# Group 0's convolutions three GLU tiles behind, with four shifted operands, and three gate pairs before their branches

## The chip, the cores and the metric

One Trainium2 chip, a program on all eight cores, each with its own 2048 prompt tokens and 64 sample tokens, no exchange between cores. The time of a run is that of its slowest core, in device microseconds. Most runs agree within 0.3%, but some fall in a slower state, in which the cores of one die or both show a lower granted clock; only fast runs are compared for whole times.

A few words before the rest. **PE** is TensorE, **DVE** VectorE, **ACT** ScalarE, **SP** SyncE, which here does nothing but issue copies. **Stages** below are read from each core's trace, all eight cores, by the end of four instructions of group 0: the last write of the GLU output of tile 0 ("glu 0"), the last convolution matmul ("conv 7"), the last tile of the gated mixture ("mix") and the last residual sum of the output projection ("projection"). The profile page itself is that of the slowest core alone.

## The reference, cut to what matters

One decoder layer. Attention and a causal depthwise convolution run side by side on the same normalised input; sigmoid gates merge them; an output projection adds to the residual; an MLP follows.

```python
q, k, v, u, g = _project(_rmsnorm(x, norm1_g), w_in, b_gate)   # u = ua * sigmoid(ub): GLU, 1024 channels
ya = _prompt_attention(q, k, v, sink)
c = conv31(pad(u)) + conv_b                                    # 31 taps, one filter per channel
yc = silu(layernorm(c)) @ w_conv_o
mix = (g0 * (ya @ w_attn_o) + g1 * yc) @ w_out
h = x + mix
h = h + square(relu(rmsnorm(h) @ w_up)) @ w_down
```

## The kernel before: the parts that the argument touches

Tokens are split in three groups; group 0 has 640 columns. Only there the convolution runs on PE (later groups do it on DVE behind the MLP). A channel tile of 128 is cut in four quarters q of 32 channels. For each quarter, 32 partitions of `um` are copied to four places, shifted by i = 0 to 3 columns; eight matmuls of 128 rows and 32 columns then sum 32 taps. That takes 16 small SBUF-to-SBUF copies for each tile, all issued by SP.

```python
GROUPS = [(0, 5, 128, 0), (5, 6, 0, 0), (11, 5, 0, NSMP)]
M_OUT = list(range(8)) + [10, 11, 14, 15, 8, 9, 12, 13]      # order of the output projection's tiles
ush = [over(X[1], i * 8 * ULEN, f"ush{i}", [128, 4, ULEN], BF16) for i in range(2)]   # shifted operands
cw = [over(H, 4096 + i * 2048, ...) for i in range(2)]                                # taps
um = [over(H, 8192 + i * 2560, ...) for i in range(2)]                                # GLU output
tAH = over(H, 8 * HB, "tAH", [128, 4, WMAX], F32)            # gates held for two pairs, in H's tiles 8-11
tBH = over(H, 12 * HB, "tBH", [128, 4, WMAX], F32)           # and 12-15

def glu(m):
    ...
    if first:
        P.dma("sp", cw[m % 2][...], cwb[:, m, :]..., f"d_cw{m % 2}")
    ...                                   # 64 matmuls, Tanh on ACT, multiply on DVE into um[m % 2]
    if first:
        z = ush[m % 2]
        for i in range(4):
            for q in range(4):
                P.dma("sp", z[32 * i:32 * i + 32, q, 0:L - 3], u[32 * q:32 * q + 32, i:i + L - 3],
                      f"d_ul{m % 2}{i}{q}", merge=(i + q > 0))
...
for m in range(8):
    glu(m)
    if first and m >= 1:
        conv(m - 1)
...
if first:
    side.extend([lambda: None, lambda: None, lambda: conv(7), lambda: None, lambda: ln_stats(0)])
    side.extend([lambda m=m: ln_apply(0, m, cf[m % 2]) for m in range(8)])
```

`side` is a list of small tasks; after each gate chunk (16 matmuls, 2.17 us) one is taken. In the gates of group 0 the tasks are, first, the last conv and the layer norm; then, when those are done, the squares of group 1's input (16 loads of 384 KB through the three-tile ring `xrP`) and the residual loads into H:

```python
if first:
    for p in range(2):
        gate(p, tA, 0)
        gate(p, tB, 16)
    drain()                                                   # runs what is left in side
    begin, tasks = norm1_squares(g + 1, xrP)
    begin()
    side.extend(tasks)                                        # 33 tasks
    side.extend([lambda m=m: load_res([m]) for m in M_OUT[:12]])   # 12 tasks
    for p in range(2):
        branches(p)
for p in range(2 if first else 0, 8):
    gate(p, tA, 0); gate(p, tB, 16); branches(p)
drain()
begin, tasks = norm1_scale(g + 1, XF[...], xrP)               # reads the same 16 tiles again, during
begin()                                                       # the output projection, into the ring
side.extend(tasks)
if first:
    load_res(M_OUT[12:])
```

The helper that ends the program makes SP wait for every semaphore that the program ever used:

```python
def emit(self):
    fin = [(s, v) for s, v in self.cnt.items() if v > 0]
    self.streams["sp"].append((fin, None, None))
```

The softmax here doesn't subtract the row's maximum and nothing guards it: scores larger than these inputs give would overflow.

## Time and profile before

| | before |
|---|---|
| time, median of 4 runs | 3396.76 us (3395.22 to 3692.71; the longest run was slow) |
| cores of the profiled run | 3373.6 to 3390.5 us |
| PE busy | 3312.6 of 3390.5 us |
| conv stage (glu 0 to conv 7), median of cores | 122.8 us (115.0 to 137.5) |
| to the last mix tile | 207.1 us |
| output projection | 78.6 us (71.3 to 79.8) |

The page of the slowest core (4): busy time of PE, the granted clock in 40 slices, and the chain that ended last.

```profile
PE 3312.6 (98%) x22688; PEld 2161.1 (64%) x22688; DVE 1621.9 (48%) x2438; ACT 718.6 (21%) x1371; POOL 267.9 (8%) x475
PEclk7989999999999999999999999999999999999999
...
PE 94%; DMA 2%; DVE 2%; SPq 1%; issue 1%; ACT 0%; DVEq 0%; ACTq 0%; POOLq 0%
```

PE is the bound. A slice is 85 us long; the two with a clock under nine tenths are the first and the third (170 to 254 us). The table of stretches of the same core shows where: columns are the stretch, its length, busy us and instruction counts of each engine, the clock, the share of the DMA engines.

```profile
core 4: us, PE busy (x) PEld busy (x) DVE busy (x) ACT busy (x) POOL busy (x), PEclk, DMA share, GB/s
144.00:166.00 22.00, 18.28 (x161) 10.54 (x161) 11.08 (x10) 8.37 (x18) 6.32 (x11) 0.92 0.55 119
...
182.00:206.50 24.50, 15.95 (x184) 10.24 (x176) 7.40 (x8) 3.44 (x7) 0.53 (x1) 0.79 0.75 151
206.50:241.00 34.50, 25.88 (x261) 16.71 (x256) 5.95 (x10) 5.82 (x12) 1.05 (x2) 0.85 0.62 117
241.00:275.00 34.00, 27.98 (x273) 18.30 (x271) 6.94 (x11) 8.08 (x15) 1.06 (x2) 0.90 0.44 98
```

PE's waits between 120 and 275 us (total us, times, longest) and two conv lines of its timeline:

```profile
PE ps L157 <- DMA ush_89<-um_95: 22.7, 6, 6.7
PE ps L157 <- DMA ush_88<-um_94: 3.0, 1, 3.0
...
202.54 4.12 PE L157 MATMUL ps<-ush_89,cw_93 128*32 128x320 bf16 x61 [6.66 <-DMA ush_89<-um_95]
...
215.82 2.37 PE L157 MATMUL ps<-ush_88,cw_92 128*32 128x320 bf16 x64
```

The same conv takes 2.37 us when PE was busy before it; after a wait, its last 61 of 64 matmuls alone take 4.12 us. The timeline of SP shows why PE waits: a set of 16 shifts takes 11 to 13 us to issue, one GLU's matmuls take 9.3.

```profile
181.94 12.55 SPq L157 DMA_DIRECT2D ush_89<-um_95  x16
194.64 0.47 SPq L157 DMA_DIRECT2D cw_92<-cwb  x1
195.41 11.26 SPq L157 DMA_DIRECT2D ush_88<-um_94  x16
```

### The profile page before, as it was taken

The numbers are of one execution on the slowest core, as the hardware profiler recorded it, in microseconds if no ns is written. First come the engines' busy times: TensorE is split into PE (matmuls) and PEld (weight loads), VectorE is DVE, ScalarE is ACT, GpSimd is POOL, SyncE is SP. The second block draws the span as 40 slices with busy tenths as digits, with TensorE's granted clock in tenths as the row PEclk, the third lists the DMA queues.
The fourth block names the chain that finished last, engine by engine and source line by source line (L and its number), as shares of the span: only waits on it lengthen the run. The fifth ranks groups of instructions, "written<-read, shape, count | busy, mean of one in ns | idle before, by whom it ended". The sixth has DMA issues, their size and how long they took to land.

```text
span 3390.5 us, 59039 instructions; the slowest of 8 cores (3373.6 to 3390.5 us)
## 1 busy us (share of the span) xinstructions
PE 3312.6 (98%) x22688; PEld 2161.1 (64%) x22688; DVE 1621.9 (48%) x2438; ACT 718.6 (21%) x1371; POOL 267.9 (8%) x475
## 2 busy tenths in 40 slices
PE   6979999999999999999999999999999999999998
PEld 4556776567777775666655666666666666666667
DVE  4534333668889453225288666644542232222225
ACT  2323223321211222112242020203211230101022
POOL 0200000300000000000130000000000000000000
PEclk7989999999999999999999999999999999999999
DMA  6766997467776696858648655555778656668651
GB/s 150 143 119 135 194 188 153 84 123 140 139 142 119 118 197 141 191 110 177 123 83 158 114 102 104 104 102 112 156 165 194 111 110 112 112 109 150 109 106 70
DMA packets 88770, 446.79 MB, mean 132 GB/s; under 512 B 11024, under 2 KB 19920, under 8 KB 45648
## 3 DMA queue, kind: packets, MB, share of 16 engines
q0 software_dynamic: 48240, 349.36, 57.3%
q1 hardware_dynamic: 39968, 93.12, 9.1%
q8 instruction: 187, 3.06, 0.4%
q14 instruction: 87, 0.71, 0.1%
q10 hardware_dynamic: 288, 0.52, 0.0%
HBM read 766.65 MB, written 25.94 MB: 234 GB/s over the span
## 4 chain that ended last, share of the span: by engine, by line
PE 94%; DMA 2%; DVE 2%; SPq 1%; issue 1%; ACT 0%; DVEq 0%; ACTq 0%; POOLq 0%
PE ps L157 94%; SPq L157 1%; DMA ush_89<-um_95 1%; DVE rden_68 L157 0%; DMA wsl_49<-wst 0%; DVE rden_67 L157 0%; DVE H L157 0%; DMA xs_106<-xp 0%; DMA xrP_121<-x 0%; DMA xs_107<-xp 0%; DMA xs_105<-xp 0%; DMA ush_88<-um_94 0%; ACT TQ L157 0%; DVE XF_79 L157 0%; DVE XQ_84 L157 0%
## 5 line engine op out<-in xcount | busy, mean ns | idle before, releaser
L157 DVE TENSOR_TENSOR H<-ps,H 128x320 f32<-128x320 f32 (+4 forms) x400 | 202.7, 507 | 378.1 <-PE ps L157 377.9
L157 PE MATMUL ps<-XF_79,wsl_49 128*128 128x320 bf16 (+3 forms) x1568 | 243.2, 312 | 11.8 <-DVE XF_79 L157 6.3
L157 PE MATMUL ps<-XF_79,wsl_53 128*128 128x320 bf16 (+2 forms) x1472 | 219.6, 309 | 0.0
L157 PE MATMUL ps<-XF_79,wsl_52 128*128 128x320 bf16 (+2 forms) x1472 | 219.4, 310 | 0.0
L157 PE MATMUL ps<-XF_79,wsl_50 128*128 128x320 bf16 (+2 forms) x1472 | 217.7, 308 | 0.8 <-DVE XF_79 L157 0.5
L157 PEld LDWEIGHTS ps<-XF_79,wsl_49 128*128 128x128 bf16 x1568 | 155.1, 99 | 97.0 <-issue 26.4
L157 PE MATMUL ps<-XF_81,wsl_49 128*128 128x384 bf16 (+2 forms) x1344 | 210.2, 317 | 0.0
L157 PE MATMUL ps<-XF_81,wsl_52 128*128 128x384 bf16 (+2 forms) x1344 | 206.0, 314 | 0.0
L157 PE MATMUL ps<-XF_81,wsl_50 128*128 128x384 bf16 (+2 forms) x1280 | 200.0, 317 | 0.0
L157 PE MATMUL ps<-XF_79,wsl_51 128*128 128x320 bf16 (+2 forms) x1344 | 197.8, 307 | 0.0
L157 PE MATMUL ps<-XF_81,wsl_53 128*128 128x384 bf16 (+2 forms) x1280 | 197.4, 315 | 0.0
L157 PEld LDWEIGHTS ps<-XF_79,wsl_53 128*128 128x128 bf16 x1472 | 143.5, 98 | 73.0 <-issue 2.7
L157 PEld LDWEIGHTS ps<-XF_79,wsl_52 128*128 128x128 bf16 x1472 | 143.7, 98 | 72.1 <-issue 1.4
L157 PEld LDWEIGHTS ps<-XF_79,wsl_50 128*128 128x128 bf16 x1472 | 143.4, 98 | 71.7 <-issue 4.0
L157 PE MATMUL ps<-XF_81,wsl_51 128*128 128x384 bf16 (+2 forms) x1216 | 186.5, 314 | 0.0
L157 PEld LDWEIGHTS ps<-XF_81,wsl_49 128*128 128x128 bf16 x1344 | 132.0, 98 | 74.6 <-issue 0.4
L157 DVE SCALAR_TENSOR_TENSOR tAP<-tAP,ps 128x384 f32<-128x384 f32 (+1 forms) x64 | 34.4, 537 | 302.5 <-PE ps L157 301.6
L157 PE MATMUL ps<-XF_80,wsl_49 128*128 128x352 bf16 (+4 forms) x1184 | 178.8, 311 | 0.0
L157 PEld LDWEIGHTS ps<-XF_81,wsl_52 128*128 128x128 bf16 x1344 | 131.3, 98 | 71.3 <-issue 1.0
L157 PEld LDWEIGHTS ps<-XF_79,wsl_51 128*128 128x128 bf16 x1344 | 131.1, 98 | 63.7 <-issue 2.1
L157 PEld LDWEIGHTS ps<-XF_81,wsl_50 128*128 128x128 bf16 x1280 | 125.6, 98 | 71.3 <-issue 1.4
L157 PE MATMUL ps<-XF_80,wsl_51 128*128 128x352 bf16 (+4 forms) x1120 | 170.6, 313 | 0.0
(406 smaller groups left out, 4575.5 us busy)
## 6 DMA issues: line engine op xcount, KB each, us to landing
wsl_49<-wst POOLq DMA_DIRECT2D x66, 1024.0 KB, 8.2
wsl_50<-wst POOLq DMA_DIRECT2D x66, 1024.0 KB, 8.3
wsl_51<-wst POOLq DMA_DIRECT2D x65, 1024.0 KB, 8.3
wsl_52<-wst POOLq DMA_DIRECT2D x65, 1024.0 KB, 8.2
wsl_53<-wst POOLq DMA_DIRECT2D x65, 1024.0 KB, 8.1
xrP_121<-x SPq DMA_DIRECT2D x18, 384.0 KB, 7.6
xrP_123<-x SPq DMA_DIRECT2D x18, 352.0 KB, 5.4
H<-x SPq DMA_DIRECT2D x16, 384.0 KB, 10.2
```

The source lines that it names most:

```text
L157: i = getattr(eng, ins[0])(**ins[1])
```

## The change

Its intent: let conv m run after glu m+3 instead of after glu m+1, so that the shifts have two more GLUs to arrive. That needs four shifted operands (each now cut to `UL0`, group 0's own 672 columns, where `ULEN` was 1248); taps are asked for later, so that they do not hold up shifts on SP; convs 5, 6 and 7 move into the gates; and to have room for them, a third gate pair is done before the branches, with six instead of four gate slots, which changes the order in which H's tiles come free (`M_OUT`).

```diff
-M_OUT = list(range(8)) + [10, 11, 14, 15, 8, 9, 12, 13]
+M_OUT = [0, 1, 2, 3, 6, 7, 8, 9, 12, 13, 14, 15, 4, 5, 10, 11]
-        ush = [over(X[1], i * 8 * ULEN, f"ush{i}", [128, 4, ULEN], BF16) for i in range(2)]
+        ush = [over(X[1], i * 8 * UL0, f"ush{i}", [128, 4, UL0], BF16) for i in range(4)]
... (um likewise of length UL0)
-        tAH = over(H, 8 * HB, "tAH", [128, 4, WMAX], F32)
-        tBH = over(H, 12 * HB, "tBH", [128, 4, WMAX], F32)
+        tAH = over(H, 4 * HB, "tAH", [128, 6, WMAX], F32)
+        tBH = over(H, 10 * HB, "tBH", [128, 6, WMAX], F32)
... (the order of the weight slabs follows the gates)
+            def load_taps(m):
+                P.dma("sp", cw[m % 2][:, :, :, :], cwb[:, m, :]..., f"d_cw{m % 2}")
             def glu(m):
-                if first:
-                    P.dma("sp", cw[m % 2]...)
+                if first and m >= 2:
+                    load_taps(m - 2)
...
-                    z = ush[m % 2]
+                    z = ush[m % 4]
-                                  f"d_ul{m % 2}{i}{q}", merge=(i + q > 0))
+                                  f"d_ul{m % 4}{i}{q}", merge=(i + q > 0))
...     in conv(m), after its matmuls:
+                if m in (4, 5):
+                    load_taps(m + 2)
...
-                if first and m >= 1:
-                    conv(m - 1)
+                if first and m >= 3:
+                    conv(m - 3)
...
-                side.extend([lambda: None, lambda: None, lambda: conv(7), lambda: None, lambda: ln_stats(0)])
+                side.extend([lambda: None] + [lambda m=m: conv(m) for m in (5, 6, 7)] + [lambda: None, lambda: ln_stats(0)])
...     in gates:
-                for p in range(2):
+                for p in range(3):
                     gate(p, tA, 0)
                     gate(p, tB, 16)
                 drain()
                 begin, tasks = norm1_squares(g + 1, xrP)
...
-                for p in range(2):
+                for p in range(3):
                     branches(p)
-            for p in range(2 if first else 0, 8):
+            for p in range(3 if first else 0, 8):
```

More of the change, by code (lines that the diff above doesn't have):

```diff
@@ L23 @@
 SEQW = 36
-M_OUT = list(range(8)) + [10, 11, 14, 15, 8, 9, 12, 13]
+M_OUT = [0, 1, 2, 3, 6, 7, 8, 9, 12, 13, 14, 15, 4, 5, 10, 11]
 NK = 14
 NB = 46
-ULEN = 32 + 640 + 16 * SEQW
+UL0 = 32 + 128 * GROUPS[0][1]
 NSLOT = 5
@@ L253, in build @@
         XU = [over(X[i], 4 * HB, f"XU{i}", [128, 8, WMAX + 32], BF16) for i in range(3)]
-        ush = [over(X[1], i * 8 * ULEN, f"ush{i}", [128, 4, ULEN], BF16) for i in range(2)]
+        ush = [over(X[1], i * 8 * UL0, f"ush{i}", [128, 4, UL0], BF16) for i in range(4)]
         gtH = [over(H, i * 2048, f"gtH{i}", [128, 512], F32) for i in range(2)]
         cw = [over(H, 4096 + i * 2048, f"cw{i}", [128, 4, 8, 32], BF16) for i in range(2)]
-        um = [over(H, 8192 + i * 2560, f"um{i}", [128, ULEN], BF16) for i in range(2)]
-        tAH = over(H, 8 * HB, "tAH", [128, 4, WMAX], F32)
-        tBH = over(H, 12 * HB, "tBH", [128, 4, WMAX], F32)
+        um = [over(H, 8192 + i * 2560, f"um{i}", [128, UL0], BF16) for i in range(2)]
+        tAH = over(H, 4 * HB, "tAH", [128, 6, WMAX], F32)
+        tBH = over(H, 10 * HB, "tBH", [128, 6, WMAX], F32)
         KcT = over(X[1], 0, "KcT", [128, 2, 16, 128], BF16)
@@ L300, in bank @@
             return bank() if b in held else b
-        A, B, C = range(NK), range(NK, NB), range(NB, 110)
+        A, C = range(NK), range(NB, 110)
+        B1 = [NK + i for i in (0, 1, 2, 3, 6, 7, 4, 5, 8)] + [*range(NK + 9, NB)]
         B2 = [NK + i for i in (0, 1, 4, 2, 3, 5)] + [*range(NK + 6, NB)]
-        order = [*A, *B, *A, *C, *B2, *A, *C, *B2, *C][:-3]
+        order = [*A, *B1, *A, *C, *B2, *A, *C, *B2, *C][:-3]
         nxt = [0]
@@ L806, in front @@
             L = 32 + Mp
+            def load_taps(m):
+                P.dma("sp", cw[m % 2][:, :, :, :], cwb[:, m, :].rearrange("p (b t c) -> p b t c", b=4, t=8),
+                      f"d_cw{m % 2}")
             def glu(m):
@@ L810, in glu @@
                 wl = slab()
-                if first:
-                    P.dma("sp", cw[m % 2][:, :, :, :], cwb[:, m, :].rearrange("p (b t c) -> p b t c", b=4, t=8),
-                          f"d_cw{m % 2}")
-                else:
+                if first and m >= 2:
+                    load_taps(m - 2)
+                if not first:
                     P.op("act", "copy", out=u[:, 0:32], in_=cuT[:, m, :])
@@ L846, in glu @@
                             P.dma("sp", z[32 * i:32 * i + 32, q, 0:L - 3], u[32 * q:32 * q + 32, i:i + L - 3],
-                                  f"d_ul{m % 2}{i}{q}", merge=(i + q > 0))
+                                  f"d_ul{m % 4}{i}{q}", merge=(i + q > 0))
             def conv(m):
-                z = ush[m % 2]
+                z = ush[m % 4]
                 c_w = cw[m % 2]
@@ L942, in gate @@
                         b = fm(w, j, nT, halo + c0, n)
-                        act(t[:, jj % 4 if first and p < 2 else j, c0:c0 + n], b[:, 0:n], AF.Tanh, scale=0.5,
+                        act(t[:, jj % 6 if first and p < 3 else j, c0:c0 + n], b[:, 0:n], AF.Tanh, scale=0.5,
                             bias=hbg[:, bias + jj:bias + jj + 1])
@@ L950, in branches @@
                     jj = 2 * p + j
-                    i = jj % 4 if first and p < 2 else j
+                    i = jj % 6 if first and p < 3 else j
                     f = slice(j * 128, j * 128 + 128)
```

## The prediction

> **What bounds it.** TensorE: the busy table gives PE 98% of 3390.5 us, the chain of waits 94%. The change can win only where PE stands or runs at a low clock. Group 0's GLU/convolution stage holds most of that: in the table of stretches PE is busy 18.3 of 22.0 us (144-166 us), 16.0 of 24.5 (182-206.5), 25.9 of 34.5 (206.5-241) and 28.0 of 34.0 (241-275), at granted clocks of 0.92, 0.79, 0.85, 0.90. In the list of PE's waits, the shifted operands (ush) account for 22.7 + 3.0 us.
>
> **Cause.** Each conv(m) follows glu(m+1), 9.3 us of matmuls. Its 16 shift copies take 11.0 to 13.3 us to issue on SP (timeline, mean 12.2), and the last lands 3.8 to 8.5 us later. Every second conv therefore waits, then runs cold: 64 matmuls take 4.1 to 5.9 us instead of 2.37. The Trainium skill, "TensorE: Matmul & The Clock Gate", Part 1, says an idle window of about 3.4 us halves the clock; this trace agrees (0.58 at 202-207 us, 0.57 at 230-242).
>
> **What the change does.** It lets conv lag three GLUs behind, with four ush buffers. No operation count changes. Three gate pairs precede their branches, to make room for conv 5, 6, 7 after gate chunks of 2.17 us each.
>
> **Gain without waits.** From 145.0 us (end of glu 1), glu 2 and 3 with attention take about 24 us; five convs (2.35) and four glus (9.25) then end at 218. Four gate chunks and conv 5 to 7 end at about 233.5. Before reaches that point at 270.9 + 2.2 = 273.1. So 39.6 us is the ceiling.
>
> **What takes half of it back.** SP does not get faster. From 133.6 us it must issue 8 sets x 12.2 us plus six tap loads at 0.7: the last shift is issued near 236. The taps of conv 6 are asked for only after conv 4, in program order behind the last shifts, so conv 6 has no taps and conv 7 no operands until about 242.5, an estimate from landings of 3.1 to 9.4 us. PE arrives at 226.8 us: one wait of about 16 us, on cw, then a cold restart (about 5 us for conv 6). Conv 7 ends near 252.5 us, 20.5 us earlier than now. Two um buffers make DVE wait in glu 5 to 7 (2 to 5 us each); eight PSUM banks absorb that.
>
> **Later.** Side tasks: 45 against 40 steps (48 before), so five residual loads are drained at the gates' end. SP can start the 12 loads (34.9 us) about 48 us before the output projection, so nothing is given back there. The last normalised tile is already just in time (0.5 us PE wait at 549 us), so up to 2 us could appear.
>
> **Predicted:** 3396.6 - 20.5 = 3376 us, 80% range 3362 to 3387. Chances: faster by over 2% 0.01; within 2% 0.98; slower 0.01.
>
> **What would show it.** SP's shift sets back to back; conv 0 to 5 with no PE wait, about 2.37 us each; one long PE wait at conv 6 released by the cw DMA; conv 7's end near 252 us; the rest unchanged and shifted.
>
> **What would make it wrong.** Issue time: at 10.5 us per set the gain is about 33 us, at 13.5 about 10. Conv 6 not waiting would mean the taps' order is harmless. A PE wait on PSUM banks in glu 6 or 7 would mean the two um buffers matter. A wait on H or XF at 450-560 us would be a give-back.

## The result

3400.51 us (median of 4 runs, 3399.25 to 4015.05; the longest was slow) against 3396.76. The ratio is 1.0011, 95% interval 0.9989 to 1.0034: the same. A ratio is the mean time of one kernel's fast runs over that of the other's of the same rounds, so it is not quite the ratio of the medians. I had predicted 3376, with a range of 3362 to 3387.

So nothing was gained; yet in the conv stage the trace looks much as predicted. On the profiled core (7) the waits for shifts are gone (on the other seven too: PE's only waits for copies there are for taps, 4.5 to 6.9 us in all), the clock holds until 206 us, and the last conv ends at 252.1 us; I had said 252.5. First the stretches, then SP's timeline (sets back to back), then PE's waits between 120 and 260 us.

```profile
core 7: us, PE busy (x) PEld busy (x) DVE busy (x) ACT busy (x) POOL busy (x), PEclk, DMA share, GB/s
144.00:166.00 22.00, 21.02 (x148) 12.04 (x146) 16.54 (x14) 8.53 (x19) 8.20 (x15) 1.00 0.67 118
...
182.00:206.50 24.50, 22.55 (x243) 14.86 (x241) 5.95 (x10) 5.38 (x11) 1.06 (x2) 1.00 0.76 149
206.50:241.00 34.50, 28.05 (x313) 18.36 (x311) 5.95 (x10) 6.94 (x14) 1.06 (x2) 0.91 0.76 145
```

```profile
189.51 11.89 SPq L157 DMA_DIRECT2D ush<-um  x16
201.55 0.47 SPq L157 DMA_DIRECT2D cw<-cwb  x1
202.53 11.32 SPq L157 DMA_DIRECT2D ush<-um  x16
214.00 0.47 SPq L157 DMA_DIRECT2D cw<-cwb  x1
```

```profile
PE ps L157 <- DMA cw<-cwb: 6.7, 2, 5.6
```

The one long wait left is for taps (5.6 us), before conv 5, and that conv then takes 5.83 us cold (granted clock 0.50 from 235.8 to 241.7 us). Conv 5 and conv 7:

```profile
235.84 5.83 PE L157 MATMUL ps<-ush,cw 128*32 128x320 bf16 x64 [5.60 <-DMA cw<-cwb]
...
249.74 2.37 PE L157 MATMUL ps<-ush,cw 128*32 128x320 bf16 x64
```

Where did the gain go? Stages of all cores:

| stage, median of 8 cores (range), us | before | after |
|---|---|---|
| start to glu 0 | 132.5 | 133.5 |
| glu 0 to conv 7 | 122.8 (115.0 to 137.5) | 116.0 (114.8 to 118.7) |
| to the last mix tile | 207.1 (207.1 to 207.2) | 204.7 (204.7) |
| output projection | 78.6 (71.3 to 79.8) | 91.7 (86.8 to 95.8) |
| last 635 us (from group 2's projection to the end) | 634.0 (633.5 to 635.1) | 635.8 (635.6 to 636.3) |
| end, median of cores | 3383.1 | 3390.4 |

Two things stand out. The conv stage gained not 20.5 but 6.8 us in the median, plus 2.4 us in the next row, most of it a gate chunk that now comes before conv 7: 9.2 us together. The 137.5 us was core 4 alone, the very core whose page I had read. And the output projection lost 13.1 us. PE's waits between 440 and 580 us, before (core 4) and after (core 7):

```profile
PE ps L157 <- DVE XF_79 L157: 0.5, 1, 0.5
```

```profile
PE ps L157 <- DVE XF L157: 9.3, 3, 3.9
PE ps L157 <- DVE H L157: 6.3, 1, 6.3
```

PE waits for DVE, and DVE waits for loads: the chain of waits of the new kernel from 443 us shows two `xrP` loads that take 21 and 29 us, one after the other, where the ring has three tiles (start, length, what).

```profile
443.83 21.08 DMA xrP<-x
...
466.12 28.81 DMA xrP<-x
...
495.98 0.49 DVE H L157
...
496.72 26.25 PE ps L157 x176
```

In the old kernel the loads of this time (issued from 15 us before the last mix tile to 30 us after it) landed in 4 to 18 us on all cores. The one load that stands in its chain, near the end of the projection (core 4):

```profile
538.24 9.72 DMA xrP_121<-x
```

SP's issues and PE's first projection matmuls say when each kernel asks for its loads, before (core 4), then after (core 7):

```profile
401.96 0.33 SPq L157 DMA_DIRECT2D xrP_121<-x  x1
402.34 34.87 SPq L157 DMA_DIRECT2D H<-x  x12
...
473.77 13.89 SPq L157 DMA_DIRECT2D H<-x  x4
...
476.56 8.86 PE L157 MATMUL ps<-XF_80,wsl_52 128*128 128x320 bf16 x64
```

```profile
406.93 0.33 SPq L157 DMA_DIRECT2D xrP<-x  x1
407.31 36.33 SPq L157 DMA_DIRECT2D H<-x  x12
443.83 1.54 SPq L157 DMA_DIRECT2D xrP<-x  x3
452.58 7.07 SPq L157 DMA_DIRECT2D H<-x  x4
...
455.44 34.94 PE L157 MATMUL ps<-XF,wsl 128*128 128x320 bf16 x256
```

The stretches from the residual loads to the projection tell what differs, before (core 4) and after (core 7); the last but one figure is the DMA share.

```profile
402.00:438.00 36.00, 36.00 (x262) 25.69 (x261) 13.61 (x17) 11.95 (x20) 2.11 (x4) 1.00 0.97 218
438.00:474.00 36.00, 36.00 (x268) 25.93 (x266) 9.10 (x19) 5.50 (x11) 2.11 (x4) 1.00 0.85 176
474.00:510.00 36.00, 36.00 (x268) 25.93 (x266) 18.99 (x36) 10.42 (x19) 2.11 (x4) 1.00 0.97 202
```

```profile
407.00:443.00 36.00, 36.00 (x262) 25.71 (x260) 13.44 (x17) 11.90 (x20) 2.11 (x4) 1.00 0.94 200
443.00:457.00 14.00, 14.00 (x105) 10.09 (x104) 5.81 (x12) 1.24 (x3) 1.05 (x2) 1.00 1.01 214
457.00:497.00 40.00, 33.66 (x248) 24.01 (x247) 10.64 (x19) 7.02 (x13) 2.11 (x4) 0.97 1.01 215
```

Both kernels fill the DMA engines while the twelve residual loads run, and again during the projection. Before, 36 us at a share of 0.85 lay between the two. After, the last mix tile comes 14 us after the last of the twelve was issued, and the engines stay full for over 50 us.

A full share alone does not make loads slow: in the old kernel it is 1.03 from 498 to 518 us (core 4), and the loads issued there landed in 7.5 to 11.3 us. What differs is the backlog. 10 us before the last mix tile, the loads that SP had issued and that had not landed were 0 or 1 on every core before, and 4 to 7 after; 10 us after that tile they were 2 or 3 before, and 4 to 7 after.

### The profile page after: what moved, and what is told of

The parts are those of the page before. It is cut to its first block, busy times and chain, and to the rows that moved or that the text cites. A ratio compares the mean times of both kernels' runs of the same rounds, so it can differ in the third digit from the quotient of the medians.

```text
span 3398.2 us, 59063 instructions; the slowest of 8 cores (3378.2 to 3398.2 us)
## 1 busy us (share of the span) xinstructions
PE 3316.6 (98%) x22688; PEld 2161.8 (64%) x22688; DVE 1622.8 (48%) x2438; ACT 718.7 (21%) x1371; POOL 267.8 (8%) x475
## 4 chain that ended last, share of the span: by engine, by line
PE 90%; DMA 3%; SPq 3%; DVE 2%; issue 1%; ACT 0%; DVEq 0%; ACTq 0%
PE ps L157 90%; SPq L157 3%; DMA xrP<-x 2%; DMA H<-x 1%; DVE rden L157 1%; DMA vec<-vecs 1%; DVE H L157 0%; DVE XF L157 0%; DMA cw<-cwb 0%; ACT TQ L157 0%; DVE R L157 0%; DVE XQ L157 0%; ACT tI L157 0%; DVE wpr L157 0%; SPq L154 0%
## 5 line engine op out<-in xcount | busy, mean ns | idle before, releaser
L157 PE MATMUL ps<-XF,wsl 128*128 128x384 bf16 (+4 forms) x19392 | 2909.9, 312 | 28.7 <-DVE XF L157 20.2
L157 PEld LDWEIGHTS ps<-XF,wsl 128*128 128x128 bf16 x19392 | 1892.3, 98 | 1043.4 <-issue 66.2
L157 DVE SCALAR_TENSOR_TENSOR acc<-XU,vec,acc 128x768 f32<-128x768 bf16 (+1 forms) x480 | 440.1, 946 | 1.1 <-ACT acc L157 1.1
L157 ACT ACTIVATE XF<-rt 128x320 bf16<-128x320 f32 (+2 forms) x384 | 189.8, 496 | 1129.9 <-DVE rt L157 1129.8
L157 POOL DMA_DIRECT2D wsl<-wst x327 | 173.5, 531 | 2900.4 <-PE ps L157 2839.3
L157 DVE SCALAR_TENSOR_TENSOR rt<-ps,LM 128x320 f32<-128x320 f32 (+2 forms) x384 | 200.1, 523 | 401.6 <-PE ps L157 398.3
L157 DVE TENSOR_TENSOR S<-S,TQ 128x320 f32<-128x320 f32 (+4 forms) x164 | 91.3, 557 | 126.4 <-ACT TQ L157 126.4
L157 PE MATMUL ps<-XU,wsl 128*128 128x320 bf16 (+2 forms) x768 | 122.4, 313 | 0.0
L157 PE MATMUL ps<-XQ,wsl 128*128 128x320 bf16 (+2 forms) x768 | 122.4, 313 | 0.0
L157 DVE RECIPROCAL rden<-rden 128x512 f32<-128x512 f32 (+1 forms) x36 | 114.3, 3175 | 3.7
L157 POOL TENSOR_SCALAR_AFFINE_SELECT PT<-PT 128x512 bf16<-128x512 bf16 x128 | 78.5, 644 | 103.5 <-ACT PT L157 103.5
```

Of the source, the lines that this page charges most:

```text
L157: i = getattr(eng, ins[0])(**ins[1])
```

## The experiments

Theory (**crowding**): the third gate pair delays the start of the side loads by 26 us of matmul work (three gate-and-branch pairs of 26 us instead of two), while the projection that follows stays where it was. The loads, which have to pass the same 16 DMA engines as the weights (from 400 to 500 us of the changed kernel the weights' queue takes 66% of them and SP's 30%, core 7), no longer drain before the projection's own loads begin. Rivals: a **deadline** (something that doesn't move with the earlier stages holds the projection, and any earlier gain is swallowed), the new **order** of the residual tiles, or the earlier end of the convs.

On the first chip of the experiments die 0 ran at a clock of 0.94 to 0.95 in all profiled runs, so those whole times decide nothing. I read cores 4 to 7 (clock 0.986 to 0.993), in e3 only cores 4 and 5, whose clock falls to 0.81 only from 2466 us on, and repeated e1 and e3 elsewhere. On the later chips some runs were slow too; the medians quoted there are of all runs. Where I call a kernel faster, its interval lies wholly below 1. Stage times are of one execution each.

### e1: the conv lag, with two gate pairs

```diff
-            for p in range(3 if first else 0, 8):      # and the other gate lines, tAH, tBH, M_OUT, slab order
+            for p in range(2 if first else 0, 8):      # as before
```

> The convolution part of the change alone (lag of three, four shift buffers), with two gate pairs first and the old residual order. Stages are medians over the eight cores: end of glu 0 to end of conv 7 (before 122.8, after 116.0 us), on to the last mix tile (207.1, 204.7), on to the last residual sum of the output projection (78.6, 91.7). Theory (crowding of loads): the third gate pair squeezed the side loads into 26 us less matmul work before the output projection, so here conv stage 116 +- 2 as after, output projection 78 +- 3 as before, whole kernel about 9 us (0.3%) faster than before. Rival (deadline): the output projection is held by something that does not move with the earlier stages, so it takes 78.6 + 9 = 88 or more here too and the whole kernel stays within 2 us of before.

Measured on cores 4 to 7: conv stage 114.7 to 118.7, mix 204.7, projection 79.5 to 81.4 us. Crowding holds, the deadline falls: the conv stage is as short as in the changed kernel and the projection takes its old time. The repeat:

> e1 again on another chip, for the whole time in the fast state: conv stage 116, last mix 205, output projection 79 to 81, end stage 636; sum about 6 us in the stages less 2 at the end, ratio to before 0.998 to 0.999.

It took 3396.14 us against 3406.1, ratio 0.9976 (0.9962 to 0.9990), a little better than expected; conv stage 118.3, projection 81.5, last stage 636.1 us. The change without its third gate pair is thus faster than the kernel before, by a quarter of a per cent.

### e2: the gate part alone

```diff
-                for p in range(2):                     # kernel before, gate(p), branches(p)
+                for p in range(3):                     # with tAH, tBH, M_OUT and slab order of after
```

> The gate part of the change alone: three gate pairs first, new residual order, the convs one GLU behind as before. Theory (crowding): conv stage as before, 123 +- 3 us, output projection about 92 +- 3 us as after, because the side loads start 26 us of matmul work later; whole kernel about 12 us (0.35%) slower than before. Rival (the conv lag or its earlier finish causes the loss): output projection 78 +- 3 us and the whole kernel equal to before.

Cores 4 to 7: conv stage 115.2 to 127.5, mix 207.2, projection 94.8, 90.0, 80.3 and 97.8 us. The loss appears without the conv lag. One core of the four (6) lost little, and its loads landed in a median of 15.7 us instead of 24 to 27; why it escaped I did not find. Cores 0 to 3, on the slow die, took 76.8 to 78.8 us there; I do not use them.

### e3: the side tasks one gate pair earlier

```diff
-                for p in range(3):
+                for p in range(2):
                     gate(p, tA, 0)
                     gate(p, tB, 16)
                 drain()
                 begin, tasks = norm1_squares(g + 1, xrP)
                 begin()
                 side.extend(tasks)
                 side.extend([lambda m=m: load_res([m]) for m in M_OUT[:12]])
+                gate(2, tA, 0)
+                gate(2, tB, 16)
```

> The whole change, but the side tasks (squares of the next group, residual loads) are started before the third gate pair instead of after it, which gives them 48 steps again. Theory (crowding): conv stage 116 as after, output projection 78 +- 3, landings of the loads at the start of the output projection 5 to 15 us instead of 21 to 34, whole kernel about 9 us faster than before. Rival (the order in which the residual tiles come, or six gate slots, causes the loss): output projection stays at 92 +- 3.

On the two undisturbed cores the projection took 77.4 and 79.2 us. The repeat:

> The kernel of e3 again, because the first chip had one die slow in all its runs. Crowding theory: conv stage 116, output projection 78 +- 3 on undisturbed cores, ratio to before 0.997 to 0.999 (9 us of gain in the stages, 2 us lost at the end, see e9). Rival: output projection 92, ratio 1.000 to 1.003.

All cores: conv stage 116.4, mix 205.0, projection 78.1 (77.7 to 80.1) us; time 3393.86 against 3409.14, ratio 0.9956 (0.9918 to 0.9993). PE's waits of the stretch 440 to 560 us (slowest core, 2) are down to one:

```profile
PE ps L157 <- DVE XF L157: 2.1, 1, 2.1
```

Here the order of the tiles, the six slots and the three pairs are all kept, only the start of the loads moves, and the loss is gone; so is the backlog (0 or 1 loads in flight 10 us before the last mix tile, on all cores). The order is acquitted.

### e5: half the residual bytes

```diff
+                    h = M // 2 if first else M
+                    if first:
+                        P.op("dve", "memset", ap=H[:, m, h:M], constant=0.0)
-                    P.dma("sp", H[:, m, 0:M], xin[g][:, m, halo:W], f"d_h{m % 4}")
+                    P.dma("sp", H[:, m, 0:h], xin[g][:, m, halo:halo + h], f"d_h{m % 4}")
```

> The whole change, but in group 0 only half of each residual tile is loaded, the other half is set to zero (a wrong result on purpose): the same number and order of loads, 3.1 MB less to move. If the loads crowd each other by bytes: landings near 455 to 475 us fall from 21 to 34 us to under 15, output projection 80 +- 4 us. If it is the number or the order of loads, or the wait of the issuing queue: output projection stays at 92 +- 3.

Its output is wrong, which doesn't matter for the time. (The expectation's 3.1 MB is a slip: a residual tile of group 0 is 320 KB, so 16 halves are 2.6 MB.) Cores 4 to 7: projection 74.8, 76.2, 71.7 and 75.5 us. The number and order of the loads are those of the change, so it is their bytes that hurt; 10 us before the last mix tile 0 or 1 loads were in flight. The median landing of the SP loads around the start of the projection goes with it; the table takes, for each core, the median of the loads issued from 15 us before the last mix tile to 30 us after it, and then the median over the cores used.

| kernel | loads land in, us | projection, us |
|---|---|---|
| before | 10.4 | 78.6 |
| after | 23.8 | 91.7 |
| e1 on its second chip | 11.0 | 81.5 |
| e2 (cores 4 to 7) | 25.4 | 92.4 |
| e3 on its second chip | 11.6 | 78.1 |
| e5 (cores 4 to 7) | 8.4 | 75.2 |

### e4: half of the shifts from ACT

The second question: what bounds the changed conv stage, which still takes 116 us where I had reckoned about 100 without waits?

```diff
+                    P.streams["act"].append((P._deps("act", set(), P.keys(z[:, :, :])), None, None))
-                            P.dma("sp", z[32 * i:32 * i + 32, q, 0:L - 3], ...
+                            P.dma("act" if q % 2 else "sp", z[32 * i:32 * i + 32, q, 0:L - 3], ...
```

(The first line makes ACT wait for the former users of the buffer; without it ACT's copies would not wait for them.)

> The whole change, but half of the 16 shift copies of each glu are issued from ACT instead of all from SP. Theory (the changed conv stage is bound by SP's issue of shifts, 8 sets of 12 us one behind the other): the stage from glu 0 to conv 7 falls from 116 to about 102 us, every conv without a PE wait. The output projection, still crowded, stays at 92 +- 4. Rival (the DMA engines, not the issuing queue, set the pace of the shifts): conv stage stays within 3 us of 116, landings stretch instead.

Conv stage 112.1 (109.0 to 114.7), projection 96.3 us. A miss by 10 us, and between the two theories. A set is now issued in 5.0 to 7.4 us instead of 10 to 14, and the issue of each set starts within 1 us of the end of its GLU; in the change the last set started 5.2 us after it (median). The last copy of a set lands 7.0 us after the end of the set's issue in the median (change: 4.1, from 1.3 to 8.8). The Trainium skill, "DMA: Bandwidth & Descriptors", "Issuing engines are not separate DMA queues", says that copies started by several engines run on the same 16 DMA engines and that a second issuer saves only the issue time. This trace agrees in part: the issue of a set became 6 us shorter, the time from its first issue to its last landing only 3 us (median 15.8 to 12.9). That the last shift of all lands just 3 us sooner after the first is issued (101.1 us instead of 104.3) says nothing of the DMA engines: each set waits for its GLU, and from GLU 0 to GLU 7 pass 88.9 us.

What is left is a wait for `cw`, 2.9 to 5.3 us on five of the eight cores: the tap loads queue behind the shifts on SP (on core 6 it comes before conv 6). And there is a new one: on every core PE waits 1.6 to 3.2 us for `gtH`, a tile that ACT writes, and ACT now issues copies too; in the change there was no such wait.

### e11 and e12: taps not behind shifts, all shifts on SP

```diff
-        cw = [over(H, 4096 + i * 2048, f"cw{i}", [128, 4, 8, 32], BF16) for i in range(2)]
+        cw = [over(t, o, f"cw{i}", [128, 4, 8, 32], BF16) for i, (t, o) in
+              enumerate(((H, 4096), (H, 6144), (X[1], 21504), (rden[0], 0)))]
                 if first and m >= 2:
                     load_taps(m - 2)
+                    if m >= 6:
+                        load_taps(m)                   # e11; in e12: load_taps(m) in every glu instead
... (in both, conv no longer calls load_taps)
```

> The whole change and only the four tap buffers added: shifts all on SP. Theory: conv 5 no longer waits for its taps, conv 7 waits only for the last shifts, which SP issues by about 236 us; conv stage 116 to 107 +- 3 us; output projection still crowded, 92 +- 5. If SP's issue alone is the bound, as predicted: conv stage within 3 us of 116.

Conv stage 113.3 (110.2 to 119.7), projection 98.3 us. A miss, partly of my making: the taps of conv 5 were still asked for in glu 7, behind a set of shifts, and PE still waited for `cw` on all eight cores (4.4 to 9.1 us). So:

> The whole change, with four tap buffers and each conv's taps asked for with its own glu, ahead of that glu's shifts (e11 moved the taps of conv 6 and 7 only, those of conv 5 still queued behind a set of shifts, which was a slip of its design). All shifts on SP. Theory (two bounds one behind the other: taps that queue behind shifts, then the last shifts themselves): no wait for cw, conv 5 and 6 with at most 3 us of wait, conv 7 waits for its shifts, conv stage 108 +- 3 us against 116 of the change and 104.6 of e10; output projection crowded, 92 to 98 us. If taps are harmless: conv stage within 3 us of 116.

Conv stage 113.9 (109.7 to 120.4), projection 100.0 us. A miss again: by the letter of the expectation 113.9 is within 3 us of 116, where "taps are harmless" was to be read, and so was e11. The stage's time does not separate the readings; the waits do. No wait for taps is left on any core, and the wait has moved to the shifts (0.2 to 13.5 us, on all eight cores), most of it at conv 7; SP asks for the last set 6.4 us after GLU 7 has ended (median). PE's waits of core 4:

```profile
PE ps L157 <- DMA ush<-um: 8.2, 3, 5.0
```

So the two bounds lie close behind each other. Taking either away alone gains 2 to 4 us (e12, e4), which single runs on different chips, with cores up to 10 us apart, do not show clearly; what names the bounds is which wait is left, and e10 below, which takes both away.

### e9: a shorter closing wait

```diff
-        fin = [(s, v) for s, v in self.cnt.items() if v > 0]
+        fin = [(s, self.cnt[s]) for s in sorted(self.last)]      # semaphores of copies to outputs only
```

> Before, with its closing wait on the output copies alone instead of on every semaphore of the program. After has 32 semaphores more than before, and SP takes 0.05 us for each satisfied wait of the closing list (trace). Theory: the time from the last PE matmul to the end of the span, 14.0 us before and 16.0 after, falls here to 12.5 us or less, the rest of the kernel unchanged; 1 to 4 us of the whole. Rival (the end is set by the landing of the last output copy): it stays at 14 us.

The last stage is 631.2 us (before 634.0), and from the last PE matmul to the end 11.5 to 12.5 us. Before, the last output copy landed 1.6 to 2.9 us before the end of the span, after 4.5 to 4.9, here 0.6. The two buffers more of the change bring 32 semaphores, and SP's waits at the end follow each other at 0.05 us: 32 x 0.05 = 1.6 of the 1.8 us that the last stage lost in the change. Of the whole, the 2.8 us gained drown in the noise (ratio 1.000, 0.9955 to 1.0045): the profiled run's conv stage happened to take 126.5 us.

### e8 and e10: a version with all three repairs

e8 is the change with e4's two queues, e9's closing wait, and the side loads begun still earlier:

```diff
+                begin, tasks = norm1_squares(g + 1, xrP)
+                side.append(begin)
+                side.extend(tasks)                     # behind the layer norm's tasks
                 for p in range(3):
                     gate(p, tA, 0)
                     gate(p, tB, 16)
-                drain()
-                begin, tasks = norm1_squares(g + 1, xrP)
-                begin()
-                side.extend(tasks)
```

> A version meant to beat both: the change, with shifts issued from SP and ACT by halves, with the squares of the next group started right after the layer-norm tasks in the first gates (so that the side loads have 62 steps), and with a final wait on the output copies alone. If all three theories hold: conv stage 102 +- 3, last mix 205, output projection 74 +- 4, end stage 631 to 634 instead of 636; whole kernel 27 to 34 us (0.8 to 1.0%) faster than before. If the gain of an earlier stage is given back in a later one again, under 10 us.

3378.67 us against 3409.14, ratio 0.9919 (0.9880 to 0.9958). Conv stage 112.3 (expected 102: the taps again), mix 204.7, projection 78.5 (expected 74), last stage 632.5. The gain is 0.8%, some 28 us.

e10 adds e11's four tap buffers, with its order of tap loads:

> e8 with four tap buffers, so that the taps of conv 6 and 7 are asked for in glu 6 and 7, ahead of the last shifts. Theory (in e4 and e8 the only wait left in the conv stage is for taps that queue behind the shifts): the wait of 6 to 10 us before conv 6 and its cold matmuls vanish, conv stage 112 to about 102 +- 3 us; last mix 204.7 after it; the output projection 78 +- 5; whole kernel 6 to 10 us faster than e8, ratio to before near 0.989. Rival (conv 6 waits for the shifts themselves): conv stage stays within 3 us of 112.

3375.92 us (3375.16 to 3379.2) against 3406.1, ratio 0.9919 (0.9904 to 0.9934). Conv stage 104.6, as expected: with both bounds gone at once the stage falls by 11.4 us against the change. No core waits for taps or shifts; PE's waits on the slowest (6):

```profile
PE ps L160 <- ACT gtH L160: 3.2, 1, 3.2
PE ps L160 <- DVE XQ L160: 2.0, 1, 2.0
```

Projection 79.6 us, last stage 632.3. The whole is not shown to be faster than e8: they ran on different chips, and each has the same ratio to the runs of before beside it. The median of the cores' ends in the profiled runs (3365.8 and 3370.5) points to 5 us.

## Why the prediction was wrong, point by point

- **The mechanism of the conv stage: right, with some luck in the number.** SP issues eight sets back to back, no conv waits for shifts, and what remains is a wait for taps that queue behind shifts. But I said "one wait of about 16 us, on cw" before conv 6; on the profiled core it was 5.6 us, before conv 5, whose taps also queue behind a set. Convs 2 to 4 took 3.3 to 3.4 us where I had 2.37. That conv 7 still ended at 252.1 us there, predicted 252.5, is partly luck: several errors cancelled. That SP's queue bounds the stage was right, but its shifts and its taps are two bounds (e4, e12): 2 to 4 us each alone, 11.4 us together (e10).
- **The size of the gain: wrong, a term of the sum.** "Conv 7 ends near 252.5 us, 20.5 us earlier than now": the "now", 271 us, was the slowest core's page. Its conv stage took 137.5 us, the median core's 122.8. The term measures 9.2 us in the median (6.8 in the stage, 2.4 in the next). The slow core is no fixed one: in e9, with the same conv stage, core 4 took 117.7 us and core 0 134.4, and the median was 126.5, so the 6.8 is itself uncertain by some 4 us (an estimate from 122.8 and 126.5). And the metric could not have gained 20 by it either: core 6 ended at 3390.3 us, 0.2 us before core 4, with a conv stage of 124.9.
- **"Nothing is given back there": wrong, the step that failed.** I had counted when SP may issue the residual loads and how long twelve of them took, and found 48 us for 35. The count was right (SP issued them from 407 to 443 us, and the projection's first matmul came at 455.4). What I left out is what the loads share with others: the DMA engines were full while they ran, and in the old kernel the 36 us after them were when the engines caught up: no core had more than one of SP's loads in flight 10 us before the last mix tile, after the change 4 to 7. Between the last squares load and the projection lay 74.6 us before (402.0 to 476.6) and 48.5 after (406.9 to 455.4); taking these 26 us out turned landings of 10 us into 24 and cost 13.1 us in the projection (medians). e1 and e3 remove the loss by moving the loads' start, e2 makes it alone, e5 removes it by halving bytes.
- **The small margin: seen, but undersized.** I noted that the last normalised tile was "already just in time" and allowed 2 us. On other cores than the one I read, the old projection already took 78 to 80 us where the fastest took 71.3.
- **"The rest unchanged": nearly.** The last stage lost 1.8 us through 32 more semaphores in the closing wait (e9).

The account of the medians: +1.0 before glu 0 (where nothing changed), -6.8, -2.4, +13.1, +1.8 at the end make +6.7; the cores' median end moved by +7.3. The kernel's time, its slowest core, moved by 3.8, within the interval around no change.

Two things stay open. The projections of e4, e11 and e12 (96 to 100 us) are longer than that of the change (91.7) and than I had expected, though only the conv stage was touched; they ran on other chips, and I have not separated the two. And the projection of e10 still takes 79.6 us against 71.3 on the best core of before; crowding is the likely cause, since e5 had 71.7 to 76.2, but I did not test it there.

## What to carry to other kernels

When work is reordered to close a gap, list what the moved work used to pace: a side task that starts later takes its loads with it, and a stretch in which PE is full and nothing waits can still be the time in which the DMA engines catch up. Read a stage's length from every core before its gap is counted as a gain; the page of the slowest core is chosen for being slow. And where a wait has two causes queued one behind the other, removing one only renames it: remove both in one run before judging either.

## What the Trainium skill lacked or had wrong

- "TensorE: Matmul & The Clock Gate", Part 1: nothing wrong. The halved clock after an idle window is as the page says: 0.50 granted after a wait of 5.6 us (changed kernel, core 7). Conv matmuls, which run four at a time, then followed each other at 0.27 us a group of four, warm 0.14. The conv took 5.83 us instead of 2.37, more than double, as its first three matmuls came singly, 0.44 us apart.
- "DMA: Bandwidth & Descriptors", "Issuing engines are not separate DMA queues", calls the issue time usually small relative to the copy. For one shift that holds here too (0.56 us to issue, 5.7 us to landing, medians of `ush_88` before). What the page does not say is that issues on one queue add up: 16 copies of 42 KB took SP 11 to 13 us, and the last landed 1.3 to 7.9 us after the end of that. A second issuer halved the issue time, and a set took 12.9 us to land instead of 15.8.
- The same page, "Anatomy of one DMA", gives a fixed 2 us and a term by bytes (its fit is for another issuing path). No page that I read tells what a backlog does to landings: loads of 320 and 384 KB landed in 10.4 us in the median with 0 or 1 of SP's loads in flight 10 us before the last mix tile, and in 23.8 us with 4 to 7.
- No page that I read has the cost of waits that are already satisfied (the nearest I found is the time to read a semaphore): 0.05 us each on SP at the end of this program, 2.8 us in all that a shorter list saved.
